# Decays of a gated recurrence: sums of logs by a scan along the tokens instead of products with a matrix of levels

## The chip, the cores and the metric

The kernel runs on one core of one Trainium2 chip. The metric is the device time of one execution in microseconds (us). Three executions of the kernel before took 2516.08, 2517.4 and 2520.63 us; the median is 2517.4 us. The engines are named as in the profile: PE (matrix products), PEld (its weight loads, beside PE), DVE (VectorE), ACT (ScalarE), POOL (GpSimd), SP (the queue that issues DMAs).

## The reference

A decoder of two layers on 256 tokens with 2048 channels. Layer 0 mixes by eight HGRN2 heads (key width 128) beside eight heads of FoX attention, layer 1 by four GLA heads (key width 256, value width 512); each layer ends in a SwiGLU FFN, and each sub-layer is normalised and modulated by a vector `c`. HGRN2 and GLA are the same recurrence with other gates:

```python
cum = jnp.cumsum(gc, axis=-2)                       # logs of the gates, summed along the tokens
diff = cum[..., :, None, :] - cum[..., None, :, :]
decay = jnp.where(causal, jnp.exp(jnp.where(causal, diff, 0.0)), 0.0)
scores = jnp.einsum('bhtd,bhsd,bhtsd->bhts', qc, kc, decay)
o_intra = jnp.einsum('bhts,bhse->bhte', scores, vc)
# HGRN2: gc = log(max(forget, 1e-30)); GLA: gc = log_sigmoid(...) / 16
```

The score of query t and key s is thus a sum over channels of q, k and exp of the sum of the logs between s and t.

## The kernel before

The tokens are two tiles of 128. Weights come by DMA in pieces; ACT casts each to a high part (`hi`, L166) and DVE takes the rest as a low part (`lo`, L168), in four buffers. PE multiplies the activations by them in fp32r, three matmuls of 128x512 for each product (hi, lo, hi: L189 to L191), twelve in a piece. The stream of these products, `drive` (L221), is what the kernel mainly does; `acc_A`, `acc_B`, `acc_C` are the sums of the HGRN2, FoX and GLA projections. DVE also forms the sums of the modulation, one instruction of 128x2048 at L108 (`mod`), one per piece times a rate, which is highest (1.05) beside the FoX projections.

The steps of the mixers are jobs: `run_jobs(quota())` issues some of them between two pieces, so that a job is through before its deadline, a count of pieces from the table TICKS (L31). A scheduler with a simulated timeline then sets the order of the instructions in each engine's queue. DVE, ACT and PE each run their queue in order: an instruction that waits holds up all behind it.

A head's scores are made by halving the 128 tokens, at seven levels of 64, 32, ... 1 tokens. At a level a pair of tokens is split by the middle of its block, and the sum of logs between them is that from the key to the middle plus that from the middle to the query. Each level thus needs, for each channel and token, exp of one sum of logs. `decays` (L448) makes them for a token tile t and 128 channels i, with an eighth block, the sums to the end of the tile (t = 0) or from its beginning (t = 1): the logs `lf`, split in high and low part, are multiplied by `lvl`, a constant matrix of zeros and ones of 128 x 9*128, into two PSUM tiles `ex` of 128x512 (L454), and ACT takes Exp of each (L455). The result, `dec`, has the channel on the partition and the tokens along the row. `factors` (L465) multiplies it on DVE by the transposed keys (`kd`) and queries (back into `dec`). `scores` (L490) multiplies these on PE level by level into `sc`, `cross` (L496, L499) gives `cx`, the scores between the tiles and of each token with itself. `pick` copies `sc` into the full score tile `st` (ACT L514 for the two largest levels, DVE under a mask L522 for the others; `cx` by L504). `output` (L529 to L532) multiplies `st` by the values into `po`. ACT takes squares of `po` (L624), DVE and ACT form a root (L283 to L288), and L630 gives the head's output.

In HGRN2 a unit u = 0 to 3 holds two heads; its two score tiles are st_79 and st_80. Its job has for each head the steps s0 (transposes of q and k) to s6 (copies into `st`), then the output. The gates' L562 and L563 make the split logs. In GLA `gla_gates` makes the logs of a unit, L831 and L832 split them, and `gla_scores` calls `decays` four times.

`decays` is called 16 times for HGRN2 (8 heads, 2 tiles) and 16 times for GLA (4 units, 2 tiles, 2 halves of the channels).

The step of a FoX unit named below is L768: it makes the output gate `g_B` from the sum `acc_B` and is its last reader, so that the sum's buffer is free for the next product behind it.

Of the kernel before, what the change touches and what calls it, by code (L numbers as in the profile page):

```python
# [1354 lines left out]
```

## Time and profile before

| | us |
|---|---|
| median of three executions | 2517.4 |
| profiled execution: span from first to last instruction | 2515.9 |
| PE busy | 2450.4 (97%) |
| PEld busy | 2025.2 (80%) |
| DVE busy | 1771.8 (70%) |
| ACT busy | 1160.2 (46%) |
| POOL busy | 89.4 (4%) |

The page states no time of the profiled execution beside its span. The HGRN2 heads run from about 152 to 400 us of the span, the GLA heads from about 1347 to 1695. The rows are read as follows: `out<-in` are the names of the tiles an instruction writes and reads, then come shape and count; a time in square brackets is the idle time of the engine ahead of it, with what ended it. Matmul durations overlap, so the step from one start to the next tells what one takes of PE's time; busy time counts overlaps once.

### The profile page before, as it was taken

What the parts mean: (1) busy time and instruction counts of PE and PEld (TensorE: products, weight loads), DVE (VectorE), ACT (ScalarE), POOL (GpSimd) and SP (SyncE); (2) the same over time, 40 slices, a digit from 0 to 9 for tenths busy, and PEclk for the clock granted to TensorE, in tenths of its full rate; (3) what the DMA queues carried; (4) which work ended last, traced back from release to release, by engine and by line L of the source; (5) the groups of instructions that cost most, each with busy time, mean ns of one, the idle gap of its engine ahead of it and who ended that gap; (6) DMA issues with size and microseconds to landing.
All of it is one profiled execution on the core that took longest, in us unless ns stands there. A gap on an engine that the chain in (4) does not pass through costs nothing.

```text
span 2515.9 us, 28838 instructions
## 1 busy us (share of the span) xinstructions
PE 2450.4 (97%) x11316; PEld 2025.2 (80%) x11316; DVE 1771.8 (70%) x1975; ACT 1160.2 (46%) x1600; POOL 89.4 (4%) x174
## 2 busy tenths in 40 slices
PE   5899999999999999999999999999999999999999
PEld 3678887887888888888888888888788888888887
DVE  6986887877688767766777777777676545554555
ACT  4365555545434444344345545554544344344443
POOL 0000000000000000000000000000000000000000
PEclk9999999999999999999999999999999999999999
DMA  9973767885899878777776566677477555555554
GB/s 379 422 272 140 274 257 292 340 319 216 287 349 357 317 281 293 287 277 293 287 277 226 202 243 233 242 256 283 169 296 254 191 194 184 196 188 186 199 185 149
DMA packets 93850, 647.49 MB, mean 257 GB/s; under 512 B 10417, under 2 KB 10993, under 8 KB 16401
## 3 DMA queue, kind: packets, MB, share of 16 engines
q1 hardware_dynamic: 70290, 476.59, 52.1%
q0 software_dynamic: 23424, 169.07, 18.1%
q8 instruction: 88, 1.44, 0.2%
q14 instruction: 48, 0.39, 0.0%
HBM read 641.39 MB, written 4.23 MB: 257 GB/s over the span
## 4 chain that ended last, share of the span: by engine, by line
PE 92%; DVE 6%; ACT 1%; issue 0%; DMA 0%; SPq 0%; ACTq 0%; DVEq 0%
PE acc_F L191 13%; PE acc_F L190 13%; PE acc_F L189 13%; PE acc_G L189 6%; PE acc_G L191 6%; PE acc_G L190 6%; PE acc_C L191 4%; PE acc_C L189 4%; PE acc_C L190 3%; DVE mod_s L108 3%; PE acc_B L189 2%; PE acc_B L190 2%; PE acc_B L191 2%; PE acc_O L189 2%; PE acc_O L191 2%; PE acc_O L190 2%
## 5 line engine op out<-in xcount | busy, mean ns | idle before, releaser
L168 DVE TENSOR_TENSOR lo<-raw_F,hi 128x1024 fp32r<-128x1024 f32 x352 | 429.4, 1224 | 296.9 <-ACT hi L166 296.8
L166 ACT CAST hi<-raw_F 128x1024 fp32r<-128x1024 f32 x352 | 370.5, 1053 | 478.3 <-PE acc_F L191 430.0
L191 PE MATMUL acc_F<-hi,hT_f 128*128 128x512 f32 x1408 | 551.3, 392 | 1.4 <-DVE hT_f L355 1.4
L189 PE MATMUL acc_F<-hi,hT_f 128*128 128x512 f32 x1408 | 548.4, 390 | 1.8 <-ACT hT_f L354 1.8
L190 PE MATMUL acc_F<-lo,hT_f 128*128 128x512 f32 x1408 | 548.5, 390 | 0.0
L108 DVE SCALAR_TENSOR_TENSOR mod<-mod,silu_c 128x2048 f32<-128x2048 f32 x160 | 365.4, 2285 | 11.1 <-DMA mod<-in_mod_w_dram 11.1
L168 DVE TENSOR_TENSOR lo<-raw_G,hi 128x1024 fp32r<-128x1024 f32 x176 | 214.2, 1222 | 138.3 <-ACT hi L166 138.1
L191 PEld LDWEIGHTS acc_F<-hi,hT_f 128*128 128x128 f32 x1408 | 264.4, 188 | 56.6 <-DVE hT_f L355 3.0
L189 PEld LDWEIGHTS acc_F<-hi,hT_f 128*128 128x128 f32 x1408 | 264.5, 188 | 56.1 <-ACT hT_f L354 2.2
L166 ACT CAST hi<-raw_G 128x1024 fp32r<-128x1024 f32 x176 | 185.4, 1054 | 268.6 <-PE acc_G L191 224.8
L190 PEld LDWEIGHTS acc_F<-lo,hT_f 128*128 128x128 f32 x1408 | 264.3, 188 | 55.2
L189 PE MATMUL acc_G<-hi,ct_f 128*128 128x512 f32 x704 | 273.5, 389 | 1.6 <-DVE res_G L403 1.6
L191 PE MATMUL acc_G<-hi,ct_f 128*128 128x512 f32 x704 | 274.4, 390 | 0.0
L190 PE MATMUL acc_G<-lo,ct_f 128*128 128x512 f32 x704 | 273.8, 389 | 0.0
L168 DVE TENSOR_TENSOR lo<-raw_C,hi 128x1024 fp32r<-128x1024 f32 x96 | 116.8, 1222 | 58.4 <-ACT hi L166 58.0
L189 PEld LDWEIGHTS acc_G<-hi,ct_f 128*128 128x128 f32 x704 | 132.2, 188 | 29.6 <-DVE res_G L403 2.4
L189 PE MATMUL acc_C<-hi,hT_n 128*128 128x512 f32 x384 | 154.3, 402 | 0.9 <-ACT hT_n L354 0.9
L190 PEld LDWEIGHTS acc_G<-lo,ct_f 128*128 128x128 f32 x704 | 132.2, 188 | 27.4
L191 PEld LDWEIGHTS acc_G<-hi,ct_f 128*128 128x128 f32 x704 | 132.2, 188 | 27.2
L191 PE MATMUL acc_C<-hi,hT_n 128*128 128x512 f32 x384 | 150.5, 392 | 0.7 <-DVE hT_n L355 0.7
L190 PE MATMUL acc_C<-lo,hT_n 128*128 128x512 f32 x384 | 150.9, 393 | 0.0
L166 ACT CAST hi<-raw_C 128x1024 fp32r<-128x1024 f32 x96 | 100.7, 1052 | 94.7 <-PE acc_C L191 88.4
(335 smaller groups left out, 3424.0 us busy)
## 6 DMA issues: line engine op xcount, KB each, us to landing
raw_F<-in_ffn_w_in_dram SPq DMA_DIRECT2D x176, 1024.0 KB, 4.9
mod<-in_mod_w_dram POOLq DMA_DIRECT2D x160, 1024.0 KB, 5.2
raw_G<-in_ffn_w_out_dram SPq DMA_DIRECT2D x88, 1024.0 KB, 4.9
raw_C<-in_gla_w_in_dram SPq DMA_DIRECT2D x48, 1024.0 KB, 6.0
mod_s<-in_mod_w_dram SPq DMA_DIRECT2D x32, 1024.0 KB, 10.6
raw_B<-in_ab_w_in_dram SPq DMA_DIRECT2D x32, 1024.0 KB, 5.9
raw_s<-in_start_w_dram SPq DMA_DIRECT2D x16, 1024.0 KB, 8.8
raw_A<-in_ab_w_in_dram SPq DMA_DIRECT2D x16, 1024.0 KB, 5.0
```

The source lines that it names most:

```text
L108: nc.vector.scalar_tensor_tensor(tile, tile, 1.0, silu_c, ALU.mult, ALU.mult, accum_out=modc[l, part][:, j:j + 1])
L166: nc.scalar.copy(out=hi, in_=w)
L168: env["lo"] = nc.vector.tensor_tensor(lo, w, hi, ALU.subtract)
L189: nc.tensor.matmul(o, a_hi, w_hi, start=(kt == 0), stop=False)
L190: nc.tensor.matmul(o, a_hi, w_lo, start=False, stop=False)
L191: nc.tensor.matmul(o, a_lo, w_hi, start=False, stop=(kt == last))
```

## The change

The sums of logs are no longer made on PE. The logs are put with the channel on the partition and the tokens along the row, and one instruction on DVE (`tensor_tensor_scan`) sums them along the tokens, from zero at each tile (`reset` is 0 in the first column of a tile and 1 elsewhere). The result is `cum`. For each level below the largest a DVE instruction subtracts the sum at the middle of the block from that at the token; the largest level and the eighth block come from ACT, with the sum as a bias. ACT takes the absolute value, and then Exp of all eight blocks at once, with the scale that GLA's logs had been multiplied by. The positions of the blocks (POS) become the same for both tiles, so that the keys of tile 1 are multiplied in one instruction, not two.

In HGRN2 the step s0 gets two transposes of the logs for each head (into the PSUM tile `lT`) and the scan; the split of the logs is dropped, and the maximum stays. In GLA the gate's pre-activation `z` is made transposed, by the same products with the operands exchanged, so that no transposes are added; two scans for each unit take the place of the scale and the split. The matrix `lvl`, its load and its copy go. The rest of the diff takes out comments.

```diff
         def decays(self, t, i):
             dec = self.pool.tile([P, 8, P], F32, tag="dec", name=f"dec_{self.name}_{t}_{i}")
-            for part in range(2):
-                c0 = ORDER[t][part] * P
-                ps = ps_mix(f"ex_{self.name}_{t}_{i}_{part}")
-                for w in range(2):
-                    nc.tensor.matmul(ps, self.lf[:, t, w, i * P:(i + 1) * P], lvl[:, c0:c0 + 512], start=(w == 0), stop=(w == 1))
-                nc.scalar.activation(dec[:, part * 4:part * 4 + 4, :].rearrange("p a b -> p (a b)"), ps, AF.Exp)
+            c = self.cum[i][:, t * P:(t + 1) * P]
+            for b in LEVELS[1:]:
+                src = c.rearrange("p (n w) -> p n w", w=2 * b)
+                nc.vector.tensor_tensor(dec[:, POS[b], :].rearrange("p (n w) -> p n w", w=2 * b), src,
+                                        src[:, :, b - 1:b].to_broadcast([P, 64 // b, 2 * b]), ALU.subtract)
+            if t == 0:
+                nc.scalar.activation(dec[:, 0, :], c, AF.Abs, scale=-1.0, bias=c[:, P - 1:P])
+            else:
+                nc.scalar.activation(dec[:, 0, :], c, AF.Abs)
+            nc.scalar.activation(dec[:, 1, :], c, AF.Abs, scale=-1.0, bias=c[:, 63:64])
+            nc.scalar.activation(dec[:, 2:, :], dec[:, 2:, :], AF.Abs)
+            nc.scalar.activation(dec, dec, AF.Exp, scale=-self.scale)
             self.dec[t, i] = dec
...
             else:
-                mul(kd, 0, 3, kT)
-                mul(kd, 4, 7, kT)
+                mul(kd, 1, 7, kT)
                 mul(dec, 0, 8, qT)
...
             nc.scalar.activation(key, sp, AF.Exp)
-            nc.vector.tensor_scalar(f[:, :, 0], l0, LOG_MIN_FORGET, None, ALU.max)
-            nc.vector.scalar_tensor_tensor(f[:, :, 1], l0, LOG_MIN_FORGET, f[:, :, 0], ALU.max, ALU.subtract)
+            nc.vector.tensor_scalar(l0, l0, LOG_MIN_FORGET, None, ALU.max)
...
         def s0():
+            cum = env["pool"].tile([P, 2 * P], F32, tag="cum", name=f"cum_A{u}{h}")
+            pl = ps_mix(f"lT_A{u}{h}")
+            for t in range(2):
+                nc.tensor.transpose(pl[:, t * P:(t + 1) * P], e["lf"][:, t, h * P:(h + 1) * P], ident)
+            nc.vector.tensor_tensor_scan(cum, reset, pl[:, :2 * P], 0.0, ALU.mult, ALU.add)
             r = Recurrence(env["pool"], e["qg"][:, :, h * P:(h + 1) * P], e["k"][:, :, h * P:(h + 1) * P],
-                           e["lf"][:, :, :, h * P:(h + 1) * P], 1, f"A{u}{h}")
+                           [cum], 1.0, 1, f"A{u}{h}")
...
-            for t in range(2):
-                nc.tensor.matmul(z[:, t], env["glT"][:, t * P:(t + 1) * P], gup, start=True, stop=True)
-            sp = pool.tile([P, 2, 256], F32, tag="gt", name=f"sp_C{u}")
+            z = ps_mix(f"z_C{u}").rearrange("p (i t) -> p i t", i=2)
+            for i in range(2):
+                nc.tensor.matmul(z[:, i], gup[:, i * P:(i + 1) * P], env["glT"], start=True, stop=True)
...
         def s1():
-            nc.vector.tensor_scalar(f[:, :, 0], c["sp"], 1.0 / 16.0, None, ALU.mult)
-            nc.vector.scalar_tensor_tensor(f[:, :, 1], c["sp"], 1.0 / 16.0, f[:, :, 0], ALU.mult, ALU.subtract)
+            for i in range(2):
+                nc.vector.tensor_tensor_scan(cum[:, i], reset, c["sp"][:, i], 0.0, ALU.mult, ALU.add)
```

Three places of the order follow. The first is DVE's queue at the second head of unit 3, before: `dec_A_0_0_2404` and `dec_A_1_0_2413` are that head's decays, which come from ACT, `lo` are low parts for the stream.

```order
L168 TENSOR_TENSOR lo_3001<-raw_B_1_2846,hi_3000 128x1024
L108 SCALAR_TENSOR_TENSOR mod_3_1_3016,modc_3_85<-mod_3_1_3016,silu_c 128x2048
L168 TENSOR_TENSOR lo_3028<-raw_B_2_2891,hi_3027 128x1024
L465 TENSOR_TENSOR kd_A_0_0_2422<-dec_A_0_0_2404,qkTs_A_0_2386 128x896
L465 TENSOR_TENSOR kd_A_1_0_2446<-dec_A_1_0_2413,qkTs_A_0_2386 128x384 x2
L465 TENSOR_TENSOR dec_A_0_0_2404<-dec_A_0_0_2404,qkTs_A_0_2386 128x896
L465 TENSOR_TENSOR dec_A_1_0_2413<-dec_A_1_0_2413,qkTs_A_0_2386 128x1024
L168 TENSOR_TENSOR lo_3054<-raw_B_2_2891,hi_3053 128x1024
```

And now, from the scan of this head (`cum_A_2428`) on; st_79 is the score tile of the head ahead of it.

```order
L585 SCALAR_TENSOR_TENSOR cum_A_2428<-reset,lT_A_2429 128x256
L168 TENSOR_TENSOR lo_3268<-raw_B_1_3086,hi_3267 128x1024
L108 SCALAR_TENSOR_TENSOR mod_3_5_3286,modc_3_85<-mod_3_5_3286,silu_c 128x2048
L529 COPY_PREDICATED st_79<-lmask,sc_A_2376 128x16x8
L455 TENSOR_TENSOR dec_A_0_0_2456<-cum_A_2428 128x128 x6
L455 TENSOR_TENSOR dec_A_1_0_2467<-cum_A_2428 128x128 x6
L168 TENSOR_TENSOR lo_3297<-raw_B_1_3086,hi_3296 128x1024
L511 COPY_PREDICATED st_79<-lmask,cx_A_2397 128x256
L473 TENSOR_TENSOR kd_A_0_0_2478<-dec_A_0_0_2456,qkTs_A_0_2438 128x896
L529 COPY_PREDICATED st_79<-lmask,sc_A_2390 128x32x4
L473 TENSOR_TENSOR dec_A_0_0_2456<-dec_A_0_0_2456,qkTs_A_0_2438 128x896
L473 TENSOR_TENSOR kd_A_1_0_2502<-dec_A_1_0_2467,qkTs_A_0_2438 128x768
```

The two tiles' twelve subtractions and the scan now stand on DVE between the logs and the products of L473 (L465 before), and the mask copies of the head ahead stand among them.

The second place is PE's queue at the scores of the same head. Before, 34 products stand between the last `ex` of this head and these scores, the last three of them shown:

```order
L189 MATMUL acc_B_2979<-hi_3027,hT_s_602 128x512
L190 MATMUL acc_B_2979<-lo_3028,hT_s_602 128x512
L191 MATMUL acc_B_2979<-hi_3027,hT_s_602 128x512
L490 MATMUL sc_A_2480<-dec_A_0_0_2404,kd_A_0_0_2422 128x64 x4
L490 MATMUL sc_A_2480<-dec_A_1_0_2413,kd_A_1_0_2446 128x64 x4
L490 MATMUL sc_A_2521<-dec_A_0_0_2404,kd_A_0_0_2422 128x64 x2
L490 MATMUL sc_A_2521<-dec_A_0_0_2404,qkTs_A_0_2386 128x64
```

Now, where 23 products and four transposes of q and k (L434, L435) stand between the transposes of the logs, `lT_A_2429`, and the scores:

```order
L190 MATMUL acc_B_3034<-lo_3174,hT_s_787 128x512
L191 MATMUL acc_B_3034<-hi_3173,hT_s_787 128x512
L434 MATMUL qkT_A_0_2433<-ident,qg_A_2190 128x128
L435 MATMUL qkT_A_0_2433<-ident,k_A_1966 128x128
L434 MATMUL qkT_A_0_2433<-ident,qg_A_2190 128x128
L435 MATMUL qkT_A_0_2433<-ident,k_A_1966 128x128
L497 MATMUL sc_A_2535<-dec_A_0_0_2456,kd_A_0_0_2478 128x64 x4
L497 MATMUL sc_A_2576<-dec_A_0_0_2456,kd_A_0_0_2478 128x64 x2
L497 MATMUL sc_A_2576<-dec_A_0_0_2456,qkTs_A_0_2438 128x64
```

The transposes and the scores stand closer together than `ex` and the scores did.

The third place follows on PE: the unit's output. Before, the products of st_80 (`po`) stand 32 products behind the last scores of the head, and those of st_79, ahead of them, directly behind a `cx`:

```order
L496 MATMUL cx_A_2528<-dec_A_1_0_2413,kd_A_0_0_2422 128x128
L499 MATMUL cx_A_2528<-qkTs_A_0_2386 128x128 x2
L532 MATMUL po_A_2585<-v_A_1926,st_79 128x128
L529 MATMUL po_A_2585<-v_A_1926,cs_A_2354 128x128
L530 MATMUL po_A_2585<-v_A_1926,st_79 128x128
L189 MATMUL acc_B_2979<-hi_3027,hT_s_602 128x512
L190 MATMUL acc_B_2979<-lo_3028,hT_s_602 128x512
```

Now the output of both heads stands directly behind the last scores, and the first product of the next sum, `acc_B_3273`, directly behind that:

```order
L503 MATMUL cx_A_2583<-dec_A_1_0_2467,kd_A_0_0_2478 128x128
L506 MATMUL cx_A_2583<-qkTs_A_0_2438 128x128 x2
L539 MATMUL po_A_2640<-v_A_1967,st_79 128x128
L536 MATMUL po_A_2640<-v_A_1967,cs_A_2401 128x128
L537 MATMUL po_A_2640<-v_A_1967,st_79 128x128
L539 MATMUL po_A_2640<-v_A_1967,st_80 128x128
L536 MATMUL po_A_2640<-v_A_1967,cs_A_2587 128x128
L537 MATMUL po_A_2640<-v_A_1967,st_80 128x128
L189 MATMUL acc_B_3273<-hi_3197,hT_s_244 128x512
```

And DVE's queue there, before, with the step L768 that frees a sum of FoX:

```order
L108 SCALAR_TENSOR_TENSOR mod_3_5_3231,modc_3_85<-mod_3_5_3231,silu_c 128x2048
L286 SCALAR_TENSOR_TENSOR rsu_A_2601<-hr_A_2584 128x4
L168 TENSOR_TENSOR lo_3242<-raw_B_1_3031,hi_3241 128x1024
L287 TENSOR_TENSOR rsu_A_2601<-rsu_A_2601,rsm_A_2600 128x4
L768 SCALAR_TENSOR_TENSOR g_B_3198<-acc_B_2979,g_B_3198 128x512
L288 SCALAR_TENSOR_TENSOR hr_A_2584<-rsu_A_2601,hr_A_2584 128x4
```

and now, behind the last mask copies of st_80:

```order
L529 COPY_PREDICATED st_80<-lmask,sc_A_2576 128x64x2
L529 COPY_PREDICATED st_80<-lmask,sc_A_2576 128x128
L283 TENSOR_SCALAR rsm_A_2655<-hss_A_2638 128x4
L286 SCALAR_TENSOR_TENSOR rsu_A_2656<-hr_A_2639 128x4
L287 TENSOR_TENSOR rsu_A_2656<-rsu_A_2656,rsm_A_2655 128x4
L288 SCALAR_TENSOR_TENSOR hr_A_2639<-rsu_A_2656,hr_A_2639 128x4
L778 SCALAR_TENSOR_TENSOR g_B_3253<-acc_B_3034,g_B_3253 128x512
L640 SCALAR_TENSOR_TENSOR o_A_2663<-po_A_2640,hr_A_2639,qg_A_2190 128x128 x2
```

The steps of the root (L283 to L288) and L768 (L778 now) stood among `lo` and `mod` and now stand together. Over the eight heads of HGRN2 the products that stand between `lT` and the first scores number, in the order of the program, 60, 51, 74, 72, 78, 75, 60 and 23. The scores of GLA have 53 to 80 products between the scans and the scores. Of the units' outputs, those of st_80 in units 0, 2 and 3 stand directly behind the scores of the second head now; before, 2, 26 and 32 products stood between.

## Rows read from the trace of the kernel before

**Rows 1.** The page, part 1 (busy time, share of the span and instructions of each engine) and the shares by engine of part 4 (the chain that ended last).

```profile
PE 2450.4 (97%) x11316; PEld 2025.2 (80%) x11316; DVE 1771.8 (70%) x1975; ACT 1160.2 (46%) x1600; POOL 89.4 (4%) x174
...
PE 92%; DVE 6%; ACT 1%; issue 0%; DMA 0%; SPq 0%; ACTq 0%; DVEq 0%
```

**Rows 2.** Busy time of the engines by stretch of the span, in us; in brackets the instructions, then the granted TensorE clock, the busy share of the DMA engines and GB/s. 152:400 holds the HGRN2 heads of layer 0, 1347:1695 the GLA heads of layer 1, 273:300 is the 27 us with the highest VectorE share.

```profile
152.00:400.00 248.00, 240.04 (x1242) 203.68 (x1241) 197.47 (x271) 135.02 (x265) 12.47 (x24) 0.99 0.65 239
1347.00:1695.00 348.00, 346.53 (x1677) 285.60 (x1678) 254.15 (x334) 184.69 (x282) 12.14 (x23) 1.00 0.64 233
273.00:300.00 27.00, 27.00 (x140) 22.88 (x139) 24.21 (x30) 16.06 (x23) 2.11 (x4) 1.00 0.76 268
```

**Rows 3.** What PE waited for in 152 to 400: engine, line, for whom; us in total, times, longest.

```profile
PE acc_B L189 <- DVE g_B L768: 4.3, 2, 4.1
...
PE po_A L532 <- DVE st L522: 1.1, 1, 1.1
```

**Rows 4.** PE in order of time in layer 1: start us, us. The matmuls between the two are left out; the second shown starts 17 steps behind the first.

```profile
1454.01 0.39 PE L190 MATMUL acc_C<-lo,hT_n 128*128 128x512 f32 x1
...
1457.86 0.39 PE L189 MATMUL acc_C<-hi,hT_n 128*128 128x512 f32 x1
```

**Rows 5.** The two lines of `decays`: instructions of L454 and of L455, with least, median and largest duration in ns, first and last start.

```profile
L454 PE MATMUL ex_A<-lvl,lf_A x64: 389/397/484, 166.2 to 370.5; 128*128 128x512 f32 x64
L454 PE MATMUL ex_C<-lvl,lf_C x64: 389/397/477, 1393.8 to 1657.8; 128*128 128x512 f32 x64
...
L455 ACT ACTIVATE dec_A<-ex_A x32: 585/598/616, 168.4 to 371.0; 128x512 f32<-128x512 f32 x32
```

**Rows 6.** PE in order of time at the scores and transposes of a head: start us, us.

```profile
184.79 0.39 PE L490 MATMUL sc_A<-dec_A,kd_A 128*128 128x64 f32 x2
185.01 0.39 PE L490 MATMUL sc_A<-dec_A,qkTs_A 128*128 128x64 f32 x2
...
185.96 0.27 PE L433 MATMUL qkT_A<-ident,qg_A 128*128 128x128 f32 x1
186.07 0.27 PE L434 MATMUL qkT_A<-ident,k_A 128*128 128x128 f32 x1
```

**Rows 7.** VectorE by line and shape: busy us, mean ns of one, and the idle time before.

```profile
L108 DVE SCALAR_TENSOR_TENSOR mod<-mod,silu_c 128x2048 f32<-128x2048 f32 x160 | 365.4, 2285 | 11.1 <-DMA mod<-in_mod_w_dram 11.1
...
L168 DVE TENSOR_TENSOR lo<-raw_B,hi 128x1024 fp32r<-128x1024 f32 x64 | 78.1, 1223 | 25.6 <-ACT hi L166 25.6
...
L522 DVE COPY_PREDICATED st<-lmask,sc_A 128x128 f32<-128x128 int32 x40 | 14.2, 356 | 3.7 <-ACT st L514 2.7
...
L465 DVE TENSOR_TENSOR dec_A<-dec_A,qkTs_A 128x1024 f32<-128x1024 f32 x8 | 9.8, 1219 | 0.0
L465 DVE TENSOR_TENSOR kd_A<-dec_A,qkTs_A 128x896 f32<-128x896 f32 x8 | 8.7, 1087 | 2.2 <-ACT dec_A L455 2.2
...
L465 DVE TENSOR_TENSOR kd_A<-dec_A,qkTs_A 128x384 f32<-128x384 f32 x16 | 8.3, 552 | 0.0
...
L983 DVE TENSOR_TENSOR hT_s<-tm_s,hT_s 128x256 fp32r<-128x256 f32 x16 | 6.7, 419 | 12.0 <-ACT hT_s L982 12.0
...
L504 DVE COPY_PREDICATED st<-lmask,cx_A 128x256 f32<-128x256 int32 x8 | 3.6, 449 | 2.5 <-ACT cs_A L502 2.1
...
L563 DVE SCALAR_TENSOR_TENSOR lf_A<-l_A,lf_A 128x512 fp32r<-128x512 f32 x4 | 2.7, 686 | 0.0
...
L562 DVE TENSOR_SCALAR lf_A<-l_A 128x512 fp32r<-128x512 f32 x4 | 1.7, 422 | 0.0
...
L270 DVE TENSOR_TENSOR nw_fb<-nraw_fb,nw_fb 128x128 fp32r<-128x128 f32 x1 | 0.3, 294 | 0.0
```

**Rows 8.** ScalarE by line and shape: busy us, mean ns of one, and the idle time before.

```profile
L166 ACT CAST hi<-raw_B 128x1024 fp32r<-128x1024 f32 x64 | 67.6, 1058 | 70.3 <-PE acc_B L191 61.5 <-PE acc_A L191 3.9 <-issue 3.6
...
L455 ACT ACTIVATE dec_C<-ex_C 128x512 f32<-128x512 f32 x32 | 17.6, 595 | 8.7 <-PE ex_C L454 5.2 <-PE sc_C L490 3.4
...
L472 ACT COPY kc_C<-kd_C 128x128 f32<-128x128 f32 x8 | 2.3, 293 | 0.3 <-DVE kd_C L465 0.3
```

**Rows 9.** VectorE in order of time: start us, us, one row for instructions on end of a line (x3).

```profile
370.81 2.02 DVE L465 TENSOR_TENSOR kd_A<-dec_A,qkTs_A 128x896 f32<-128x896 f32 x3
```

**Rows 10.** Stretches as in rows 2, and behind the dots PE in order of time at the second of them.

```profile
213.00:222.00 9.00, 9.00 (x40) 7.30 (x40) 3.82 (x7) 6.60 (x9) 0.00 (x0) 0.86 0.28 110
...
398.00:405.00 7.00, 6.87 (x20) 5.46 (x21) 2.35 (x11) 4.71 (x23) 0.00 (x0) 0.63 0.70 288
...
398.13 0.80 PE L189 MATMUL acc_B<-hi,hT_s 128*128 128x512 f32 x1 [4.08 <-DVE g_B L768]
...
399.58 0.63 PE L189 MATMUL acc_B<-hi,hT_s 128*128 128x512 f32 x1
400.01 0.63 PE L190 MATMUL acc_B<-lo,hT_s 128*128 128x512 f32 x1
```

**Rows 11.** ScalarE in order of time ahead of the wait of rows 10: start us, us.

```profile
391.17 0.28 ACT L624 ACTIVATE oj_A<-po_A 128x128 f32<-128x128 f32 x1 [2.17 <-PE po_A L530]
...
394.10 0.58 ACT L766 COPY v_B<-acc_B 128x512 f32<-128x512 f32 x1 [1.03 <-PE acc_B L191]
...
396.67 0.63 ACT L294 ACTIVATE g_B<-g_B 128x512 f32<-128x512 f32 x1
```

**Rows 12.** The mask copies of line 522, least, median and largest ns.

```profile
L522 DVE COPY_PREDICATED st<-lmask,sc_A x40: 286/302/451, 184.8 to 384.7; 128x128 f32<-128x128 int32 x40
```

More of the change, by code (lines that the diff above doesn't have):

```diff
@@ L85, in build @@
     ident = const.tile([P, P], F32, name="ident")
-    lvl = const.tile([P, 9 * P], F32R, name="lvl")
+    reset = const.tile([P, 2 * P], F32, name="reset")
     tri = const.tile([P, 2 * P], F32R, name="tri")
@@ L485, in scores @@
                 b = LEVELS[n]
-                p = POS[t][b]
+                p = POS[b]
                 for i in range(self.nd):
@@ L495, in cross @@
             for i in range(self.nd):
-                nc.tensor.matmul(cx[:, :P], self.kc[i], self.dec[1, i][:, 3, :], start=(i == 0), stop=(i == self.nd - 1))
+                nc.tensor.matmul(cx[:, :P], self.kc[i], self.dec[1, i][:, 0, :], start=(i == 0), stop=(i == self.nd - 1))
             if diagonal:
@@ L543, in hgrn_gates @@
         v = pool.tile([P, 2, 256], F32, tag="v", name=f"v_A{u}")
-        f = pool.tile([P, 2, 2, 256], F32R, tag="lf", name=f"lf_A{u}")
         sp = pool.tile([P, 2, 256], F32, tag="gt", name=f"sp_A{u}")
-        l0 = pool.tile([P, 2, 256], F32, tag="gt", name=f"l0_A{u}")
-        env["A", u] = dict(k=key, lf=f, v=v)
+        l0 = pool.tile([P, 2, 256], F32, tag="lf", name=f"l0_A{u}")
+        env["A", u] = dict(k=key, lf=l0, v=v)
         def s0():
@@ L814, in gla_gates @@
         pool = env["pool"]
-        f = pool.tile([P, 2, 2, 256], F32R, tag="lf", name=f"lf_C{u}", bufs=1)
-        env.setdefault(("C", u), {})["lf"] = f
+        cum = pool.tile([P, 2, T], F32, tag="lf", name=f"cum_C{u}", bufs=1)
+        env.setdefault(("C", u), {})["cum"] = cum
         c = {}
@@ L855, in s0 @@
         def s0():
-            r = Recurrence(env["pool"], e["qk"][:, :, :256], e["qk"][:, :, 256:], e["lf"], 2, f"C{u}")
+            r = Recurrence(env["pool"], e["qk"][:, :, :256], e["qk"][:, :, 256:],
+                           [e["cum"][:, i] for i in range(2)], 1.0 / 16.0, 2, f"C{u}")
             e["r"] = c["r"] = r
@@ L1053, in start @@
         nc.scalar.preload_act_table_set(EXP_LN)
-        lraw = rawp.tile([P, 9 * P], F32, tag="modraw", name="lraw", bufs=2)
-        nc.gpsimd.dma_start(out=lraw, in_=a["lvl"])
-        nc.vector.tensor_copy(out=lvl, in_=lraw)
+        nc.gpsimd.memset(reset, 1.0)
+        nc.gpsimd.memset(reset.rearrange("p (t c) -> p t c", t=2)[:, :, 0:1], 0.0)
         traw = rawp.tile([P, 2 * P], F32, tag="modraw", name="traw", bufs=2)
@@ L1259, in _constants @@
 def _constants():
-    lv = np.zeros((P, 9, P), np.float32)
     u = np.arange(P)[:, None]
     j = np.arange(P)[None, :]
-    lv[:, 0] = u > j
-    for i, b in zip((1, 2, 3, 5, 6, 7, 8), LEVELS):
-        second = (j // b) % 2 == 1
-        start = (j // b) * b
-        lv[:, i] = np.where(second, (u >= start) & (u <= j), (u > j) & (u < start + b))
-    lv[:, 4] = u <= j
     mask = np.zeros((P, 7, 64), np.int32)
@@ L1278, in _constants @@
     cm[:, P:] = np.where(j > u, np.float32(-1e30), np.float32(0.0))
-    return {"lvl": lv.reshape(P, -1), "lmask": mask.reshape(P, -1), "tri": tri, "cmask": cm,
+    return {"lmask": mask.reshape(P, -1), "tri": tri, "cmask": cm,
             "ident": np.eye(P, dtype=np.float32)}
```

9 lines of the change are left out of this document (4 added, 5 removed).

## The prediction

> **What bounds the kernel now.** I read the busy times first: PE is busy for 97% of the span, and 92% of the chain that ended last is PE's [rows 1]. Then the stretches that hold the two recurrences [rows 2]: in GLA's 348 us PE is busy for all but 1.5, in HGRN2's 248 for all but 8, so PE's work is the time in both, and DVE has room: busy 197.5 of 248 us (80%) and 254.2 of 348 (73%). The list of PE's waits says what the missing time of HGRN2 is: half is one wait of 4.1 us for L768, and the scores (`sc`) are in no row [rows 3]. So the decays of before, made on PE and ACT, are early enough everywhere. The change trades PE's work for DVE's in the stretches in which DVE is fullest. DVE has been at 24.21 us in 27 without a wait of PE, 90% [rows 2]; that is what I hold it to below.
>
> The sum is made against the profiled execution's span, 2515.9 us, since no other time of it is stated; the median of the three executions, 2517.4, lies 1.5 above.
>
> **What goes from PE.** 64 matmuls of L454 in each layer [rows 5]. A matmul of 128x512 takes (1457.86 - 1454.01)/17 = 0.2265 us of PE's time [rows 4], so 128 of them are 29.0 us. Added are 16 transposes at 0.11 [rows 6], 1.8 us. In GLA the z products are the same in number and I take them at no difference. PE's gain is 27.2 us: 12.7 in layer 0, 14.5 in layer 1. PE ends nearly all of the time, so this is on the path unless PE waits.
>
> **What comes to DVE.** Each of the 32 calls adds six subtractions of 128x128, 96 a layer. The nearest row is L270's 0.294 us for the same shape; the line through L465's 384 and 1024 columns (0.552 and 1.219, 1.04 ns a column) gives 0.285 [rows 7]. Instructions on end overlap: three of 1.087 + 2 x 0.552 = 2.19 us took 2.02 [rows 9], 0.085 at each seam. So a step is 0.20, and 96 are 19.2 us. Bounds: 0.20 below, and above it the longest masked copy of that shape, 0.451 [rows 12], a step of 0.37; the broadcast operand has no row, and the subtraction is an addition like L270's, so I take 0.20. The scan has no row; as 128x256 it would be L983's 0.419 [rows 7], a step of 0.33, 8 in each layer, 2.7 us. Bounds: that, and 0.69, at which a column takes twice as long. Dropped in layer 0 are four of L562 and L563 (0.422 and 0.686, 3.8 us as steps), of which four maxima stay (1.4); GLA drops the same work. The key products of tile 1 in one instruction save 0.15 at 8 calls, 1.2 us. DVE gains 18.3 us of load in layer 0 and 16.9 in layer 1. Without PE's gain taken off, layer 0 then holds 215.8 us in 248 - 12.7 = 235 (92%), GLA 271 in 333.5 (81%). GLA stays below what DVE has done, so its gain should come whole. Layer 0 is at the edge.
>
> [...]
>
> **ACT.** Per call two Exp of 0.598 [rows 5] become two of 128x128 (0.293), one of 128x768 (0.84, between 0.598 and the 1.06 of 1024 columns) and one of 1.05 [rows 8]: 1.28 more, 20.5 a layer. ACT then holds 155.5 of 235 us in layer 0 [rows 2], and I cost it at nothing: it is idle a third of the time. Uncovered, it is the rival below.
>
> **Which wait is added.** Before, PE reached the scores without waiting. Now a head's logs go PE, DVE (scan, 12 subtractions), ACT, DVE (products), and PE has only the products between `lT` and the scores to do meanwhile. Behind the waiting scores stand all products of the stream, so each wait is lost time. I count each head's queue of DVE from its scan to the factors of tile 0, in steps: scan 0.33, 12 subtractions 2.4, `lo` 1.14, `mod` 2.2, mask copy 0.27 (L522's mean less the seam), `cx` copy 0.36, products of 128x896 1.0, of 128x768 0.87 [rows 7, 9].
> - Head 8: scan, 2 `lo`, 1 `mod`, 2 mask copies, `cx` copy, 2 products: 10.1 us. PE has 23 products and 4 transposes, 5.65. It waits 4.5; then tile 1's factors take 2.3 on DVE while tile 0's seven scores take 0.8 at 0.11 each [rows 6]: 1.5 more. 6.0 in all.
> - Head 2: 4 `lo`, 1 `mod`, three mask copies, three products and 1.5 of gate work: 15.1 against 51 products, 12.0: 3.1, and 0.3 for tile 1.
> - Head 6: 6 `lo`, 3 `mod`, three mask copies, three products: 20.2 against 75 products, 17.5: 2.7, and 0.4 for tile 1.
> - The other five have 2 to 7 us to spare (head 1: 7.0 against 14.1).
> Sum 12.5. This takes DVE to be at the scan when the logs land. Bounds: nothing, if DVE is ahead and its `lo` and `mod` are done earlier; twice that, if DVE comes late to each scan.
>
> In GLA 53 to 80 products (12 to 18 us) stand behind the scans, as against 11 to 12 us of DVE, and I count no wait.
>
> **The unit's output.** In units 0, 2 and 3 `po` now stands behind its own scores, so PE waits for the mask copies of that head: about 1 us each, as the one row of it shows (1.1) [rows 3]; that one is of unit 0 and is already in the time. Net +1.9.
>
> **The wait for L768.** Its 4.1 us were a row of ACT steps that could only start when the sum's last product was done: 394.10 to 397.3 [rows 11]. Now they pass while PE waits for head 8. But the first product of the next sum stands directly behind `po`, and L778 behind the root of `po`, which starts with ACT's squares. Bounds: two squares alone, 0.6 [rows 11], and 4.1 as before; I take 2.4, the middle. So -1.7.
>
> **The clock.** [...] A weaker fall, 0.86 over 9 us, cost 1.3 [rows 10]. [...]
>
> **Sum.** -27.2 + 12.5 + 1.9 - 1.7 + 2.6 = -11.9, so 2504.0 on the span and 2505.5 for the median: 2505. Its own range, from the waits at 4 less or 8 more: 2498 to 2513.
>
> **Rivals.**
> - *The waits are covered.* DVE idles 50 of HGRN2's 248 us [rows 2] and may reach the scans with its other work done. For it: 80% before; against it: 23 products at head 8, which no earlier `lo` lengthens. All of PE's gain and no wait: 2515.9 - 27.2 + 1.5 = 2490.
> - *DVE's backlog grows from head to head.* At 92% it is above the 90% of its fullest stretch, `lo` is late too, and each scan is reached late. Waits twice as long, 25, and falls of the clock at two more heads, 2.6: 2505.5 + 12.5 + 2.6 = 2520.6, of which the GLA part is already taken off. About no change.
> - *DVE waits for ACT, and the time gets longer.* The products of L473 wait for four activations, 2.5 us, behind ACT's casts of 1.05. What stands behind them on DVE is `lo`, for which the stream waits. If nothing covered these 2.5, layer 0's DVE would hold 215.8 + 16 x 2.5 = 256 us, at 90% 284, so +36, less GLA's 14.5 and with its 271 + 40 still under 333.5: 2538. It decides from (215.8 + 16 L)/0.9 = 248 + 14.5 + 5, L = 1.6 us a call. Against it: tile 0's activations run beside tile 1's subtractions (1.2) and a `lo` (1.14).
>
> **How the numbers follow.** A measurement of this kernel tells 0.2%, 5 us, from no change. Forecast 0.55, waits covered 0.23, backlog 0.14, waiting for ACT 0.08. Faster (below 2512.4): 0.53 + 0.23 + 0.06 = 0.82. Same: 0.02 + 0.05 = 0.07 and a little of the last, 0.09. Slower: 0.09. The range of eight in ten takes in the covered case and most of the backlog: 2489 to 2519.
>
> **What would show it.** `ex` gone, and GLA shorter by about 14 us with no wait for `sc_C`; in layer 0 waits of PE for `sc_A` at heads 2, 6 and 8, the last the longest, some 6 us; DVE at about 90% there; the subtractions near 0.29 us, the scan between 0.42 and 0.69; the wait for L778 near 2.4. I am wrong if scores wait at every head, if `lo` becomes a wait of the products, or if GLA gains less than 10.

## The result and the profile after

The changed kernel takes 2532.8 us, the median of five executions (2527.43 to 2533.59), against 2517.4, the median of five here too; the ratio over all these runs is 1.005 with a 95% interval of 1.0036 to 1.0064. It is 0.5% slower, where 2505 was forecast with a range to 2519. The profiled execution spans 2531.8 us, 15.9 more than the one before.

The page after, parts 1 and 4, as in [rows 1]:

```profile
PE 2442.2 (96%) x11204; PEld 2019.3 (80%) x11204; DVE 1807.0 (71%) x2154; ACT 1197.5 (47%) x1664; POOL 89.4 (4%) x175
...
PE 85%; DVE 7%; issue 7%; ACT 1%; DMA 1%; POOL 0%; SPq 0%; POOLq 0%; ACTq 0%; DVEq 0%
```

PE is busy for 8 us less, DVE for 35 us more, and PE's share of the chain fell from 92% to 85%. Where the time went is read from the first and last start of the output projections' products (`acc_O`, of layer 0 and of layer 1) and of GLA's (`acc_C`). Before:

```profile
L189 PE MATMUL acc_O<-hi,ct_m x256: 387/389/497, 503.2 to 1770.8; 128*128 128x512 f32 x128
```

```profile
L189 PE MATMUL acc_C<-hi,hT_n x384: 387/389/799, 1347.8 to 1681.7; 128*128 128x512 f32 x192
```

and after:

```profile
L189 PE MATMUL acc_O<-hi,ct_m x256: 387/389/799, 529.9 to 1787.1; 128*128 128x512 f32 x128
```

```profile
L189 PE MATMUL acc_C<-hi,hT_n x384: 387/389/799, 1377.5 to 1696.2; 128*128 128x512 f32 x192
```

| stretch | before | after | difference |
|---|---|---|---|
| PE's last wait for `lo_s` of the start (141.4, now 140.3) to the output projection of layer 0 | 361.8 | 389.6 | +27.8 |
| from there to GLA's first product | 844.6 | 847.6 | +3.0 |
| GLA's first product to the last one of its output projection | 423.0 | 409.6 | -13.4 |

What lies ahead of and behind these stretches is 1.5 us shorter. GLA gained about what was forecast (14.5). Nearly all of the loss is in the stretch of HGRN2 and FoX. PE's waits there, as in [rows 3]:

```profile
PE sc_A L497 <- DVE dec_A L473: 20.4, 3, 9.8
PE acc_B L189 <- DVE g_B L778: 7.7, 2, 3.9
PE po_A L539 <- ACT oj_A L634: 1.8, 2, 0.9
PE acc_B L189 <- ACT v_A L564: 1.5, 1, 1.5
PE po_A L539 <- DVE st L529: 1.4, 1, 1.4
PE acc_A L189 <- ACT v_A L564: 1.3, 1, 1.3
```

The scores, in no row before, wait 20.4 us, and L778 (L768 before) 7.7. Summed over stretches of 2 us from 142 to the output projection, PE's idle time is 34.1 us (before 8.0), and its busy time multiplied by what the granted clock lacks of 1 is 18.8 (before 4.2). With the 12.7 us less work of the forecast, 26.1 more idling and 14.6 more at the lower clock make 28.0, and the difference is 27.8.

Three places make nearly all of the idling: heads 2, 6 and 8, each with the output of its unit. PE in order of time, in the first row at head 2, then at head 6 with the output of unit 2 (start us, us, and in brackets the wait; each score is two records):

```profile
203.40 1.52 PE L497 MATMUL sc_A<-dec_A,kd_A 128*128 128x64 f32 x12 [3.42 <-DVE dec_A L473]
...
327.17 2.79 PE L497 MATMUL sc_A<-dec_A,kd_A 128*128 128x64 f32 x12 [7.21 <-DVE dec_A L473]
...
337.47 0.77 PE L539 MATMUL po_A<-v_A,st 128*128 128x128 f32 x2 [1.43 <-DVE st L529]
...
342.98 0.76 PE L189 MATMUL acc_B<-hi,hT_s 128*128 128x512 f32 x1 [3.89 <-DVE g_B L778]
...
346.96 0.63 PE L189 MATMUL acc_B<-hi,hT_s 128*128 128x512 f32 x1
347.38 0.63 PE L190 MATMUL acc_B<-lo,hT_s 128*128 128x512 f32 x1
...
348.22 0.39 PE L189 MATMUL acc_B<-hi,hT_s 128*128 128x512 f32 x1
348.45 0.39 PE L190 MATMUL acc_B<-lo,hT_s 128*128 128x512 f32 x1
```

At head 6 PE waits 7.21 us for the factors, then 1.43 for the mask copies and 3.89 for L778. The first six scores (twelve records) take 2.79 us, and the products behind them have steps of 0.43 us until 347.8, then 0.23. PE's granted clock through the place, as in [rows 2]:

```profile
320.00:330.00 10.00, 2.83 (x14) 2.86 (x14) 10.00 (x11) 1.05 (x1) 0.53 (x1) 0.71 0.88 324
330.00:340.00 10.00, 7.66 (x34) 7.10 (x33) 4.52 (x12) 2.67 (x14) 0.53 (x1) 0.50 0.59 218
340.00:350.00 10.00, 7.02 (x21) 5.55 (x22) 2.91 (x13) 7.93 (x34) 0.00 (x0) 0.59 0.00 0
400.00:410.00 10.00, 0.47 (x3) 0.50 (x3) 9.21 (x21) 4.88 (x6) 0.53 (x1) 0.64 0.89 329
410.00:420.00 10.00, 9.09 (x42) 8.82 (x43) 4.19 (x10) 1.57 (x8) 0.31 (x1) 0.50 0.11 43
420.00:430.00 10.00, 6.20 (x17) 4.77 (x17) 3.05 (x13) 6.90 (x32) 0.31 (x1) 0.50 0.01 2
```

In windows of 2 us the granted clock is 0.50 from 326 to 348 at head 6 and from 404 to 430 at head 8, the idle time between the matmuls included. What PE waits for is DVE, in order of time from the transposed logs (PE's `lT` ended at 302.3) to the factors of head 6:

```profile
302.61 2.27 DVE L108 SCALAR_TENSOR_TENSOR mod<-mod,silu_c 128x2048 f32<-128x2048 f32 x1
...
305.02 0.67 DVE L585 TENSOR_TENSOR_SCAN cum_A<-reset,lT_A 128x256 f32<-128x256 f32 x1
305.62 1.19 DVE L168 TENSOR_TENSOR lo<-raw_B,hi 128x1024 fp32r<-128x1024 f32 x1
308.34 2.29 DVE L108 SCALAR_TENSOR_TENSOR mod<-mod,silu_c 128x2048 f32<-128x2048 f32 x1 [1.53 <-DMA mod<-in_mod_w_dram]
...
310.76 2.51 DVE L455 TENSOR_TENSOR dec_A<-cum_A 128x128 f32<-128x128 f32 x12
313.19 1.22 DVE L168 TENSOR_TENSOR lo<-raw_B,hi 128x1024 fp32r<-128x1024 f32 x1
...
314.65 1.22 DVE L168 TENSOR_TENSOR lo<-raw_B,hi 128x1024 fp32r<-128x1024 f32 x1
315.79 2.28 DVE L108 SCALAR_TENSOR_TENSOR mod<-mod,silu_c 128x2048 f32<-128x2048 f32 x1
...
318.00 1.22 DVE L168 TENSOR_TENSOR lo<-raw_B,hi 128x1024 fp32r<-128x1024 f32 x1
...
319.33 1.95 DVE L473 TENSOR_TENSOR kd_A<-dec_A,qkTs_A 128x896 f32<-128x896 f32 x2
321.20 1.22 DVE L168 TENSOR_TENSOR lo<-raw_B,hi 128x1024 fp32r<-128x1024 f32 x1
322.34 2.28 DVE L108 SCALAR_TENSOR_TENSOR mod<-mod,silu_c 128x2048 f32<-128x2048 f32 x1
...
324.79 1.24 DVE L168 TENSOR_TENSOR lo<-raw_B,hi 128x1024 fp32r<-128x1024 f32 x1
325.95 2.21 DVE L473 TENSOR_TENSOR dec_A<-dec_A,qkTs_A 128x896 f32<-128x896 f32 x2
```

DVE reaches the scan 2.7 us late, behind a `mod`. Then come a `lo`, a wait of 1.5 us for a load of the modulation's weights, a `mod`, and only then the twelve subtractions (2.51 us). Five more `lo` and two `mod` stand before the factors of the queries, with which the scores start. DVE isn't idle at all but for that load. At head 8 the transposed logs are there at 394.0 (PE, first view), and DVE (second view) reaches the scan at 397.88, 3.8 us late, and loses 1.12 us to a load:

```profile
393.66 0.38 PE L584 MATMUL lT_A<-ident,l_A 128*128 128x128 f32 x2
...
409.53 2.79 PE L497 MATMUL sc_A<-dec_A,kd_A 128*128 128x64 f32 x12 [9.81 <-DVE dec_A L473]
```

```profile
397.88 0.68 DVE L585 TENSOR_TENSOR_SCAN cum_A<-reset,lT_A 128x256 f32<-128x256 f32 x1
...
400.79 2.29 DVE L108 SCALAR_TENSOR_TENSOR mod<-mod,silu_c 128x2048 f32<-128x2048 f32 x1 [1.12 <-DMA mod<-in_mod_w_dram]
```

The new instructions on DVE (least, median and largest ns), and, in the last row, what DVE idled ahead of the scans: 1.2 us in three waits for `lT`. The other five scans found their logs waiting, for 0.5 to 3.8 us:

```profile
L455 DVE TENSOR_TENSOR dec_A<-cum_A x96: 278/282/293, 171.3 to 405.4; 128x128 f32<-128x128 f32 x96
```

```profile
L585 DVE TENSOR_TENSOR_SCAN cum_A<-reset,lT_A x8: 670/679/689, 170.6 to 397.9; 128x256 f32<-128x256 f32 x8
...
PE lT_A L584: 1.2, 3
```

### The profile page after: what moved, and what is told of

Read it like the earlier page. It is cut to its first block, busy times and chain, and to the rows that moved or that the text cites. A ratio compares the mean times of both kernels' runs of the same rounds, so it can differ in the third digit from the quotient of the medians.

```text
span 2531.8 us, 28799 instructions
## 1 busy us (share of the span) xinstructions
PE 2442.2 (96%) x11204; PEld 2019.3 (80%) x11204; DVE 1807.0 (71%) x2154; ACT 1197.5 (47%) x1664; POOL 89.4 (4%) x175
## 3 DMA queue, kind: packets, MB, share of 16 engines
q8 instruction: 87, 1.43, 0.2%
## 4 chain that ended last, share of the span: by engine, by line
PE 85%; DVE 7%; issue 7%; ACT 1%; DMA 1%; POOL 0%; SPq 0%; POOLq 0%; ACTq 0%; DVEq 0%
PE acc_F L191 13%; PE acc_F L190 13%; PE acc_F L189 13%; PE acc_G L189 6%; PE acc_G L190 6%; PE acc_G L191 6%; PE acc_C L191 4%; PE acc_C L189 3%; PE acc_C L190 3%; DVE mod_s L108 3%; PE acc_O L189 2%; PE acc_O L190 2%; PE acc_O L191 2%; DVE lo_s L168 1%; PE acc_B L189 1%
## 5 line engine op out<-in xcount | busy, mean ns | idle before, releaser
L103 POOL DMA_DIRECT2D mod<-in_mod_w_dram x160 | 84.8, 530 | 1681.7 <-DVE mod L108 1471.8
```

The lines of the kernel that those rows point to most:

```text
L103: nc.gpsimd.dma_start(out=tile, in_=a["mod_w"][l, part * KT + j])
```

## The experiments

All ratios are to the kernel before, of the same chip. The runs are of several chips, on which the kernel before took 2517.4 to 2522.5 us at the median, so versions are compared by these ratios; the changed kernel's is 1.005. The diffs are cut.

**Layer 1 alone changed.** `decays`, `factors` and the gates of HGRN2 as before, `lvl` kept; `reset` lies in GLA's pool.

```diff
+HGRN_NEW = False
+GLA_NEW = True
...
+            if self.lf is not None:
...
+                               None, 1.0, 1, f"A{u}{h}", e["lf"][:, :, :, h * P:(h + 1) * P])
```

> Layer 1 (GLA) changed, layer 0 (HGRN2) as before. The two traces say that GLA's stage went from 423.0 us (1347.8 to 1770.8) to 409.6 (1377.5 to 1787.1), and that all of the loss lies in layer 0. Theory: 2517.4 - 13.4 = 2504, with no new wait of PE and the clock as before. Rival: GLA's gain was bought by what happened ahead of it (work pushed out of the late layer 0): then under 6 us, above 2511.

2503.45 us, ratio 0.9933 (0.9919 to 0.9948). PE's waits from 145 to 440 are those of [rows 3]:

```profile
PE acc_B L191 <- DVE g_B L805: 4.3, 2, 4.1
...
PE po_A L557 <- DVE st L547: 1.1, 1, 1.1
```

GLA's gain stands by itself, and this version beats both kernels. In its trace GLA's stage takes 408.0 us (1349.1 to 1757.1), 15.0 less than before.

**Layer 0 alone changed.** GLA's gates and `decays` as before, `lvl` kept.

```diff
+HGRN_NEW = True
+GLA_NEW = False
...
-                job(gla_gates(u), TICKS["gla_gates"])
+                job((gla_gates if GLA_NEW else gla_gates_old)(u), TICKS["gla_gates"])
```

> Layer 0 changed, layer 1 as before. Theory: the changed kernel plus the 13.4 us of GLA, 2546, with PE waiting for sc_A at heads 6 and 8 for 7 and 10 us and the lower clock behind each. Rival: the loss needs both parts (the matrix of levels, its load and copy stay here): under 2535.

2551.0 us, ratio 1.0122 (1.0107 to 1.0137). The loss needs only HGRN2's part; `sc_A` waits 15.2 us here. The two ratios, 0.9933 and 1.0122, multiply to 1.0054, which is that of the whole change.

**The kernel before, with work on DVE.**

```diff
                 nc.scalar.activation(dec[:, part * 4:part * 4 + 4, :].rearrange("p a b -> p (a b)"), ps, AF.Exp)
+            if self.nd == 1:
+                spare = self.pool.tile([P, 48], F32, tag="spare", name=f"spare_{self.name}_{t}_{i}", bufs=1)
+                src = self.qkT[i][:, 2 + t, :48].rearrange("p (n w) -> p n w", w=16)
+                for _ in range(10):
+                    nc.vector.tensor_tensor(spare.rearrange("p (n w) -> p n w", w=16), src,
+                                            src[:, :, 7:8].to_broadcast([P, 3, 16]), ALU.subtract)
```

> The kernel before, with DVE work added that nobody waits for: ten subtractions of 128x48 into a spare tile in each of the 16 calls of HGRN2's decays, about 1.2 us a call and 19 us in all, about what the change adds to DVE in layer 0. The decays still come from PE. Theory A, load: DVE has no room left in layer 0, lo and the factors come late, and the time grows by 15 us or more, to 2532 or above. Theory B, chain: what costs is that the scores now wait for DVE's queue from the scan on; load alone stays hidden: 2517 to 2522.

2547.3 us, ratio 1.011 (1.0095 to 1.0125). The decays still came from PE, and PE still waited for the factors, the mask copies and L774 (L768 before):

```profile
PE sc_A L496 <- DVE dec_A L471: 9.0, 2, 5.9
PE acc_B L189 <- DVE g_B L774: 7.8, 2, 3.9
PE po_A L538 <- DVE spare_A L460: 3.3, 1, 3.3
PE po_A L538 <- DVE st L528: 2.1, 1, 2.1
```

DVE was busy for 23.0 us more than before (1794.8 against 1771.8), and that cost 28 us (2547.3 less 2519.5, the kernel before in the same runs), with no scan: theory A. It isn't load alone, since the order had moved as in the changed kernel: units 0, 2 and 3 had their output directly behind their scores. How much of the waits for `po` and L774 belongs to that order isn't separated here.

**Fewer sums of the modulation beside the heads.**

```diff
-RATES = dict(A=0.3, B=1.05, O0=0.8, F0=0.5, C=0.5, O1=0.4, F1=0.4)
+RATES = dict(A=0.3, B=0.65, B2=1.2, O0=0.95, F0=0.5, C=0.5, O1=0.4, F1=0.4)
```

> The changed kernel with the sums of the modulation spread otherwise: rate 0.65 in place of 1.05 beside FoX units 0 and 1 (where HGRN2's heads 5 to 8 run), 1.2 beside units 2 and 3, 0.95 in place of 0.8 beside the output projection; the number of sums is the same. The order then has 2 lo and 1 mod between scan and factors of head 6 instead of 6 and 3, and 34 products instead of 23 ahead of the scores of head 8. Theory (the chain is stretched by what stands between on DVE): the waits for sc_A fall from 20 us to about 8, and with the clock falls behind them the time falls by 15 to 20, to 2513 to 2518. Rival (the chain PE, DVE, ACT, DVE is long by itself): less than 6 us gained, above 2527.

2523.0 us, ratio 1.0015 (1.0006 to 1.0025): by the ratios 0.35%, some 9 us, below the changed kernel, short of the 15 to 20. The waits for `sc_A` fell to 8.0 us, as forecast, with none left at head 6; those for `po` (4.4) and L778 (7.9) stayed, and the time at the lower clock too (17.8 us by the same sum).

**The sums cut short.** 32 sums over 512 of 2048 columns, in the changed kernel, and later the same in the kernel before.

```diff
+        w = 512 if (l, part) in ((0, 2), (0, 3)) else D
-        nc.vector.scalar_tensor_tensor(tile, tile, 1.0, silu_c, ALU.mult, ALU.mult,
+        nc.vector.scalar_tensor_tensor(tile[:, :w], tile[:, :w], 1.0, silu_c[:, :w], ALU.mult, ALU.mult,
```

> The changed kernel with 32 sums of the modulation (parts 2 and 3 of layer 0, which run beside HGRN2 and FoX) formed over 512 of their 2048 columns; the other three quarters of these sums are left out, their loads stay. That takes 1.6 us from each of 32 DVE instructions, some 35 us of DVE before the last HGRN2 head ends. Theory A (DVE's load delays the chain of heads): the waits for sc_A fall from 20 us to under 5 and the time by 25 or more, to 2508 or below. Theory C (the order: a unit's scores, output and the step that frees a sum stand back to back at a product's end, which stays so at units 0 and 3 here): po and g_B still wait 10 us with the lower clock behind them, and the time stays above 2515.

> The kernel before with the same 32 sums of the modulation cut to 512 of 2048 columns, the control of the run with the changed kernel (2499.3 us): three quarters of these sums are left out. Theory A (DVE's load costs time only where the chain of the heads goes through DVE, or where it runs out): only the wait for L768 and the fall behind it go, 2510 to 2516, so that the change by itself is worth 11 to 17 us when DVE has room. Rival (short sums make anything faster, by fewer stalls elsewhere): under 2505.

The changed kernel took 2499.3 us, ratio 0.9912 (0.9897 to 0.9927), the kernel before 2514.55, ratio 0.9979 (0.997 to 0.9988). By the ratios the change is worth 0.67%, some 17 us, with room on DVE. PE's waits in the first:

```profile
PE acc_B L190 <- DVE g_B L779: 8.0, 2, 4.0
PE po_A L540 <- DVE st L530: 2.5, 2, 1.5
...
PE sc_A L498 <- DVE dec_A L474: 1.2, 2, 0.7
```

The scores wait 1.2 us in place of 20.4: theory A. The waits of theory C, for `po` and L779 behind the scores, are still there, 4.0 us of them at unit 2, where 24 products stand between the scores and the output of st_80. The gain is GLA's: its stage takes 408.0 us against 423.0. The stretch of HGRN2 and FoX takes 359.9 us in both traces, since PE idles there for 14.4 us against 5.3 and loses 7.0 against 3.1 to the lower clock, by the sums used above: 13.0 us, as much as HGRN2's 12.7 of work. The kernel before, cut in the same way, has one wait for this step, of 1.2 us:

```profile
PE acc_B L190 <- DVE g_B L769: 1.2, 1, 1.2
```

**The subtractions on GpSimd.**

```diff
-                nc.vector.tensor_tensor(dec[:, POS[b], :].rearrange("p (n w) -> p n w", w=2 * b), src,
+                (nc.gpsimd if self.nd == 1 else nc.vector).tensor_tensor(dec[:, POS[b], :].rearrange("p (n w) -> p n w", w=2 * b), src,
```

> The changed kernel with HGRN2's 96 subtractions on GpSimd, which is busy for 4% of the span, in place of DVE. DVE loses 19 us in layer 0; the chain of a head keeps its steps. Theory A (load): the waits for sc_A are halved and the time falls by 10 to 20, to 2513 to 2523, if a subtraction takes GpSimd no more than 0.5 us. Theory B (length of the chain): no gain, and a loss of 12 times whatever GpSimd takes more than 0.28 us, above 2533.

2539.9 us, ratio 1.0065 (1.0048 to 1.0082): no gain, and not told from the changed kernel, whose interval overlaps. The 96 subtractions took GpSimd 0.401 us each at the median, 0.636 in the mean and up to 2.4 (the view of the line; the page warns that spans on GpSimd are rough):

```profile
L455 POOL TENSOR_TENSOR dec_A<-cum_A 128x128 f32<-128x128 f32 x96 | 57.8, 636 | 42.1 <-DVE cum_A L585 40.5 <-ACT hi L166 1.4
```

DVE lost the load and the chain grew. `sc_A` still waits 20.0 us, in five places, and the transposes of q and k 6.4 more for a scan. Since the mean is above the 0.5 us that theory A asked for, this run doesn't tell what the load alone is worth.

**Both scans at a unit's start.**

```diff
+            if h == 0:
+                for hh in range(2):
+                    nc.vector.tensor_tensor_scan(e["cum", hh], reset, pl[:, 2 * hh * P:(2 * hh + 2) * P], 0.0,
+                                                 ALU.mult, ALU.add)
+            cum = e["cum", h]
```

> The changed kernel with the logs of both heads of a HGRN2 unit transposed and scanned at the unit's start, so that the second head's chain begins with its subtractions. DVE's load is the same. Theory B (length of the chain): the second heads, 2, 6 and 8, wait 3 to 5 us less each, and the time falls by 10 or more, to 2523 or below. Theory A (load): the scans are 0.7 us each and the rest stays; under 5 us gained, 2528 to 2533.

2519.3 us, ratio 0.9991 (0.9982 to 1.0001): by the ratios 0.59%, some 15 us, below the changed kernel, with the same instructions in another order. So the length of the chain counts beside the load: theory B held here, as theory A did with the cut sums. `sc_A` waits 10.1 us (1.0, 1.6 and 7.5 at heads 2, 6 and 8), but `po` now waits 5.8 us for the mask copies at head 6. In all PE idles 5.0 us less in layer 0 and loses 5.3 less to the lower clock.

**Layer 1 changed, and the sums spread.** The edits of the first run and of the rates.

> Layer 1 changed and layer 0 as before (2503.5 us), with the sums of the modulation spread as in the run with rates 0.65, 1.2 and 0.95. Theory A: with less of them beside HGRN2's last heads the wait for L768's 4.1 us and the clock fall behind it go: 2496 to 2500. Rival: the rate of 1.2 beside FoX units 2 and 3 makes DVE late there: 2503 or more.

2513.1 us, ratio 0.9961 (0.9947 to 0.9976): the rival's time. The longest wait for L805 fell from 4.1 to 2.6 us, yet by the ratios, whose intervals just meet, the version is 0.28% slower than the first run's. That DVE is late beside units 2 and 3, as the rival has it, isn't shown: from 440 us to the output projection PE waits in neither trace, and the trace kept is of the fastest execution, 2508.0 us.

**PE kept busy at the waits.**

```diff
+            if u >= 2 and h == 1:
+                for _ in range(10):
+                    nc.tensor.matmul(junk, r.cum[0][:, :P], r.qkT[0].rearrange("p a b -> p (a b)"), start=True, stop=True)
```

> The changed kernel with PE work that nothing needs: ten matmuls of 128x512 in f32 of the scanned logs, into a spare PSUM tile, ahead of the scores of heads 6 and 8. They stand where PE waits 7 and 10 us. Theory D (the lower clock is a consequence of PE's idling and costs some 14 us of its own): the time of the waits is filled for nothing, the granted clock stays up behind them, and the time falls by 5 to 10 us, to 2523 to 2528. Rival (the granted clock falls in any case, or the chain is what lasts): the time stays at 2533 or grows by what the ten matmuls take beyond the waits.

2531.2 us, ratio 1.0045 (1.0028 to 1.0062). The time isn't told from the changed kernel's: 8.8 us of matmuls in each place cost nothing, and at head 8 the first six scores then ran at a granted clock of 1.00 (1.45 us). But the tail behind them idled as before, and the clock fell there: the mean is 0.84 from 410 to 432, and 0.83 from 320 to 350. Idle and clock sums are 20.2 and 10.8 us, and the stretch of layer 0 is 5.3 us shorter in the trace. What the lower clock costs apart from the waits that go before it isn't settled by this.

**Both gains together.** Scans at the start, with rates 0.65, 1.2 and 0.95.

> The changed kernel with both of the edits that gained: both heads' scans at a unit's start (2519.3 us) and the sums of the modulation spread as 0.65, 1.2, 0.95 (2523.0). Gains that add up: 2533 - 13.5 - 10 = 2509. If both only take away the same waits: 2517 or more. The version with layer 1 alone changed (2503.5) would stay ahead in both cases.

2516.8 us, ratio 0.9985 (0.9976 to 0.9995). The gains don't add up: the ratio isn't told from that of the scans alone, 0.9991, and `po` and L784 (L778 above) wait 13.7 us in this version too.

## Why the prediction was wrong

Of the 27.8 us between the forecast of the span (-11.9) and its measure (+15.9), 12.0 are the clock's, 7.9 the scores' waits and 5.1 those for L778; the 3.0 of the second stretch were in no term.

- *PE's gain*: right. GLA -13.4 for -14.5, with no wait for `sc_C`; in the eight other traces with GLA changed its stage takes 407.8 to 408.3 us, -15.0. HGRN2's -12.7 fits what the idle and clock sums leave.
- *DVE's new instructions*: the subtraction at 0.282 us was right, twelve in 2.51 too. The scan took 0.679, not 0.42: I took the nearest row, and the upper bound was near the truth. It is a small part: 0.26 us at each head. DVE's load in the stretch came out at 216.0 us for 215.8, but in 274 us (152 to 426) in place of 235, so that DVE was busy for 79% of it and not 92%. The scan's 0.679 is 0.26 more than L983's 0.419 for the same shape [rows 7], about what 256 columns take at the prediction's 1.04 ns.
- *Which heads wait*: right, 2, 6 and 8. Head 2 waited 3.42 us (3.4 forecast), head 6 7.21 (3.1), head 8 9.81 (6.0). The step that failed is "This takes DVE to be at the scan when the logs land". At head 6 DVE came 2.7 us late and lost 1.5 to a load; with the forecast's 2.7 for tile 0 and the scan's 0.3 that makes 2.7 + 0.3 + 2.7 + 1.5 = 7.2. At head 8 it came 3.8 late and lost 1.1: 4.5 + 0.3 + 3.8 + 1.1 = 9.7. The waits for tile 1 (0.3, 0.4 and 1.5) didn't come. I had read one score as 0.11 us, but it is two records, so tile 0's seven take 1.5 us and not 0.8, and 3.0 at a granted clock of 0.50 (327.17 to 330.19). The stream itself fills DVE there: beside head 6's 75 products, 17 us, stand six `lo` and three `mod` (the code makes one `mod` in two pieces at rate 1, not one in each), 6 x 1.14 + 3 x 2.2 = 13.4 us.
- *The unit's output and L768*: the output's wait was right (+1.9 forecast; 3.2 for 1.1 before), L768's was mis-sized. I counted one wait of 2.4 us in place of 4.1; there are two of 3.8 to 3.9, since unit 2's output ends a sum as well. In the trace and the program the reason can be read: `acc_B_3273` can start only when one of the two buffers of the sums is free. ACT read the one sum (L705) from 425.75 on, though its last product had ended by 372, since the program puts this behind all steps of HGRN2's unit 3; the other is freed by L778, which DVE starts at 423.99. So PE had no product left to do while the tail ran. Before, 45 products stood there behind the last scores. ACT's first instruction of L705 in order of time:

```profile
425.75 0.28 ACT L705 ACTIVATE qk_B<-acc_B 128x128 f32<-128x128 f32 x1 [0.40 <-DVE o_A L640]
```

- *The clock*: 14.6 us for 2.6, nearly as large a miss as that of all waits (26.1 for 12.7). No run shows the sum's +2.6: it was my estimate, from the length of one wait at each of two heads. Before, the stretch of 0.86 [rows 10] came behind two waits, of 1.07 and 1.25 us. Now, behind head 2's one of 3.42, the clock is 0.50 from 206 to 210. At head 6 three waits (7.21, 1.43 and 3.89 us) follow each other with 8.9 and 1.6 us of matmuls between, and the clock is 0.50 from 326 to 348, the products behind the last wait included. PE before, in order of time at the two waits:

```profile
209.95 0.46 PE L532 MATMUL po_A<-v_A,st 128*128 128x128 f32 x2 [1.07 <-DVE st L522]
...
212.11 0.79 PE L189 MATMUL acc_A<-hi,hT_s 128*128 128x512 f32 x1 [1.25 <-ACT v_A L558]
```

- *The rivals*: that DVE's backlog grows (2520.6, a chance of 0.14) was right in part. Five of the eight scans were reached late, and the 20.4 us of waits lie nearer to its 25 than to the forecast's 12.5, but the lateness doesn't grow from head to head (head 7's scan was on time), and no product of HGRN2's stretch waited for `lo`. Its price lacked the tail and most of the clock. That the scores' waits are covered came true only with DVE's sums cut short. DVE waiting for ACT played no part: among DVE's waits from 150 to 440 there is none of L473.
- *The range*: I set its upper end just below the one rival that let delays pass from head to head (2520.6). The 90% of a full stretch, taken as what DVE can hold, says nothing of when the work comes: heads run one after the other, each behind its own scan, and DVE's queue ran in order: at head 6 the subtractions, whose scan had ended at 305.69, stood behind a `mod` that waited 1.53 us for a load, and started at 310.76.

Open stays how much of the loss the lower clock would cost without the waits, and how much the new order of the queues costs by itself: no run changes the order alone. Open is also why the same short waits at the output projection (0.58, 0.23 and 0.67 us before; 0.57, 0.23 and 0.68 after) left the clock at 1.00 before and were followed by 0.66 from 580 to 585 after, which is about half of the 3.0 us of the second stretch. It isn't HGRN2's change: with layer 1 alone changed the clock is 0.83 from 550 to 560 (before 1.00) and the stretch takes the same 847.6 us, and with both scans at a unit's start it takes 844.4.

## What to carry to other kernels

Work that is moved from the bound engine to one with a third of its time free gains only if that time lies where the work comes: look at the stage, at what the stream itself takes of the engine there, and at which results the bound engine then needs next. A chain that goes through an in-order queue costs what stands in that queue (here six `lo` and three `mod`, and a wait of 7.21 us, at head 6), and a step that frees an accumulator is part of the chain (here two waits of 3.8 to 3.9 us for L778). Change the stages apart: here the stage with room gained 0.7% and the other lost more than that.

## What was not expected of the hardware

A scan of 128x256 on DVE took 0.679 us at the median, and a broadcast subtraction of 128x128 0.282, where the one of L270 without a broadcast took 0.294 [rows 7]. GpSimd's subtraction of the same shape took 0.401 us at the median, with single ones of 2.4. Around waits in a row (7.2, 1.4 and 3.9 us at head 6) the granted clock was 0.50 for some 20 us, from 327 to 347.8, over six scores that took 2.79 us in place of 1.45 and products with steps of 0.43 in place of 0.2265.
